# The last layer's gate: half of its contraction as seven block products

## The chip, the cores and the metric

The kernel runs on one core of one Trainium2 chip. The metric is the device time of one execution in microseconds. TensorE (PE in the profile) multiplies, VectorE (DVE) and ScalarE (ACT) do elementwise work, SyncE (SP) issues the transfers from memory.

## The reference

A two-layer decoder trunk on 512 tokens of 1024 features in float32. Layer 0 mixes tokens with a Mamba-2 SSD, layer 1 with HGRN2; each is followed by a layer norm, a squared-ReLU MLP and a second layer norm. What matters here is the end of a layer, with h of shape 512 x 1024:

```python
h = layer_norm(DEEPNORM_ALPHA * h + sq_relu_mlp(h, mlp_w1[i], mlp_w2[i]), ln_g[i, 1], ln_b[i, 1])
x = h + jax.nn.sigmoid(h @ ple_w_gate[i]) * (p[i] @ ple_w_proj[i])
```

The gate is a product of 512 x 1024 by 1024 x 1024, the projection one of 512 x 256 by 256 x 1024. The result of the last layer is the output.

## The kernel before

Tokens are cut into four chunks of 128 (c), features of the contraction into eight blocks of 128 (k), outputs into two halves of 512 (h), so that one PSUM bank holds 128 tokens x 512 outputs. Every float32 operand is split into a rounded part and a rest (`split`, `transpose_split`: a cast on ACT, line 113 or 242, and a subtraction on DVE, line 116 or 243), and `mm3` multiplies three times: hi·hi, hi·lo, lo·hi (lines 120 to 122). Weights come in units of 128 x 1024, two blocks k of one output half. `unit` takes one of three raw buffers, loads it on SP's queue (line 106), and splits it into one of six pairs whi, wlo.

The MLP's second product and a value projection of layer 1 already use the scheme of seven products for a 2 x 2 block product (`block_product`, `values4`). Sums of weight blocks (`weight_sums`, lines 333 to 341) are made by DVE in buffers r, of which there are eight; sums of token blocks are made from a plain copy of the turned rows (lines 551 to 564, `put` in lines 522 to 525).

The order on each engine is made by a scheduler that takes the instructions in the order of the code, moved ahead by the offsets of `high_priority` (LEAD = 100, SOON = 40 instructions), as their operands and buffers come free in its own model of time. Each engine then works through its list in order. Loops are unrolled.

The stage around the change, in `mlp_and_gate` for the last layer: the MLP's last block product fills acc, the rows of 512 tokens. `norm(3)` returns three things: `chunk(c)`, which normalises 128 tokens (`layer_norm`, lines 213 to 224), `transpose_split` for a chunk (two groups of four 128 x 128 transposes into the single bank pt, line 238, then the cast and the subtraction), and the row sums. Chunks 0 and 1 are normalised after the fifth product, chunks 2 and 3 after the last, in the last layer's case with no raised priority for chunks 2 and 3. Then lines 474 to 512 run the gate: for h = 0 all four projections of p first (line 482), with chunk 1's transposes between them, and for each chunk 24 matmuls into a bank pj (line 493) with the transposes of chunks 2 and 3 set between those of chunks 0 and 1. Each bank is followed by a sigmoid on ACT (line 496), a multiply by the projection and an add to acc on DVE (lines 503 and 506), and the store of 128 x 512 outputs (line 508). For h = 1 each chunk's projection comes right before its 24 matmuls; the last chunk's comes behind them, in two pieces of 256 columns, so that the last multiply, add and store are short.

Of the kernel before, what the change touches and what calls it, by code (L numbers as in the profile page):

```python
# [9 lines left out]
F32R = mybir.dt.float32r  # L10
# [34 lines left out]
def trunk(ctx: ExitStack, tc, a):  # L45
# [43 lines left out]
    def tmp(tag, shape, dt=F32):  # L89
        return mk(phase[0], shape, tag, dt, bufs=phase[2].get(tag, 1))  # L90
# [137 lines left out]
    def behind(ins):  # L228
        return tc.issue_after(ins.ins) if ins is not None else nullcontext()

    def transpose_split(src, dst, c, apart):

        sl = slice(c * P, (c + 1) * P)
        for q in range(2):
            pt = bank(psm, "pm") if apart and q else bank(pst, "pt")
            for j in range(4):
                k = 4 * q + j
                nc.tensor.transpose(pt[:, j * P : (j + 1) * P], src[:, k * P : (k + 1) * P], ident)  # L238
            v = pt.rearrange("p (j t) -> p j t", j=4)
            h = dst.hi[q][:, :, sl]  # L240
            with tc.high_priority(offset=LEAD if apart else SOON):
                nc.scalar.copy(h, v)
                turned_last[:] = [nc.vector.tensor_sub(dst.lo[q][:, :, sl], v, f32(h))]
            yield

# [34 lines left out]
                for c in range(NCH):  # L280
                    out_part(units, 4, xs, c, h, first, scale)

    def norm(i):
# [9 lines left out]
        return h_s, chunk, lambda c: transpose_split(acc[:, c, :], h_s, c, c == 3 and i % 2 == 0), sums  # L293

# [49 lines left out]
    def block_product(w, blk, lead, first, after=None, turns=None, sums=None, low=None):  # L344
# [41 lines left out]
        for f in (p1, p7, p6, p4, p5, p2, p3) if after else (p1, p2, p6, p7, p5, p4, p3):  # L386
# [4 lines left out]
                after(2), after(3)  # L391
            yield

    def mlp_and_gate(layer, h_s, last):
# [36 lines left out]
        for g, period in enumerate(PERIODS):  # L431
            if g < 4:
                tiles = hidden(g)
            if g > 0:
                if g == 4:
                    h_s, after, turned, sums = norm(2 * layer + 1)
# [11 lines left out]
        x_n = None if last else Split(8)  # L448
        rows = None if last else [tmp("blk", [P, 2, 4, 256]) for _ in range(2)]
        late = []  # L450

        def turn(h, c):

            sl = slice(c * P, (c + 1) * P)
            pt = bank(pst, "pt")
            for j in range(4):
                nc.tensor.transpose(pt[:, j * P : (j + 1) * P], acc[:, c, h * 512 + j * P : h * 512 + (j + 1) * P], ident)
            v = pt.rearrange("p (j t) -> p j t", j=4)
            hh = x_n.hi[h][:, :, sl]
            nc.scalar.copy(hh, v)  # L460
            nc.scalar.copy(rows[c // 2][:, h, :, c % 2 * P : (c % 2 + 1) * P], v)
            nc.vector.tensor_sub(x_n.lo[h][:, :, sl], v, f32(hh))

        pps = {}

        def proj(c, pu, chunk=None, cs=slice(0, T)):

            ps = pps[c] = bank(*((psj, "pj") if c > 1 and pps else (psy, "py%d" % (c % 2))))
            sl = slice(c * P, (c + 1) * P) if chunk is None else slice(chunk * P, (chunk + 1) * P)
            for k in range(2):  # L470
                ks = slice(k * 512 + cs.start, k * 512 + cs.stop)
                mm3(ps[:, cs], p_s[0][:, k, sl], p_s[1][:, k, sl], pu[0][:, ks], pu[1][:, ks], k == 0, k == 1)

        for h in range(2):
            pu = unit(a[f"wp_{layer}"][h])
            gu = [unit(a[f"wg_{layer}"][4 * h + j]) for j in range(4)]
            for c in range(NCH):
                sl = slice(c * P, (c + 1) * P)
                if h == c == 0:
                    turns = turned(1)  # L480
                    for i in range(NCH):
                        proj(i, pu)
                        if i in (1, 2):
                            next(turns)
                end = last and h == 1 and c == NCH - 1
                if h == 1 and not end:
# [9 lines left out]
                nc.scalar.activation(sg, pg, AF.Sigmoid)  # L496
                for i in range(2 if end else 1):
                    n = 256 if end else 512
                    cs = slice(i * n, (i + 1) * n)
                    if end:  # L500
                        proj(i, pu, c, cs)
                    pp = pps.pop(i if end else c)[:, cs]
                    nc.vector.tensor_mul(sg[:, cs], pp, sg[:, cs])  # L503
                    fs = slice(h * 512 + i * n, h * 512 + (i + 1) * n)
                    d = acc[:, c, fs]
                    nc.vector.tensor_add(d, sg[:, cs], d)
                    if last:
                        nc.sync.dma_start(a["out"][c * P : (c + 1) * P, fs], d)
                while late:
                    late.pop(0)()  # L510
                if not last:
                    late.append(lambda h=h, c=c: turn(h, c))
        return x_n, rows, late

    def values4(xs, rows, late):
# [791 lines left out]
```

## Time and profile before

| | us |
|---|---|
| median of 3 runs | 1415.1 (1414.85 to 1415.71) |
| the profiled execution | 1415.16 |
| its span, first to last instruction | 1413.4 |
| the last layer's gate, first projection to last matmul | 1351.3 to 1409.4 |

The profile is of one execution. Times in its rows count from the start of the span. A row of a timeline gives start, duration, engine, line of the kernel, operation, output<-inputs and shapes. A row of a group gives a count, the busy time, the mean in ns of one, and the idle time of the engine just before, with what ended it. PEld is the load of the stationary operand, which runs beside the matmuls.

### The profile page before, as it was taken

The page shows a single profiled execution, that of the slowest core. Times are in us where ns is not written, and L with a number is a line of the kernel's source. Part 1 is how long each engine was busy: PE and PEld are TensorE (multiplying, and loading weights), DVE is VectorE, ACT ScalarE, POOL GpSimd, SP SyncE. Part 2 cuts the span into 40 slices and gives each one's busy share as a digit, 9 for nine tenths or more (in the row PEclk, how much of TensorE's full clock was granted, in tenths as well). Part 3 has the DMA queues.
Part 4 walks back from the last instruction along what each step waited for, and adds up shares of the span by engine and source line. Part 5 has one row for each costly group of instructions (what it writes and reads, how often), then busy time and mean ns, then how long its engine had stood idle before and what let it go on. Part 6 is the DMA issues. An engine that isn't in the chain of part 4 may idle for free.

```text
span 1413.4 us, 20324 instructions
## 1 busy us (share of the span) xinstructions
PE 1408.5 (100%) x8013; PEld 1170.9 (83%) x8013; DVE 1057.1 (75%) x1759; ACT 750.7 (53%) x1132; POOL 1.9 (0%) x12
## 2 busy tenths in 40 slices
PE   9999999999999999999999999999999999999998
PEld 7888888888988888888888888888888888888887
DVE  7989687698977668677986577678785857667873
ACT  6766465573354444545555547655555454544641
POOL 0000000000000000000000000000000000000000
PEclk9999999999999999999999999999999999999999
DMA  8433333234434444444621421222163444444231
GB/s 304 140 120 117 108 119 107 88 100 143 151 114 134 149 136 147 137 147 164 214 85 49 134 91 61 76 91 90 44 241 105 153 145 134 149 135 162 91 119 45
DMA packets 49391, 178.02 MB, mean 126 GB/s; under 512 B 5520, under 2 KB 6288, under 8 KB 49168
## 3 DMA queue, kind: packets, MB, share of 16 engines
q1 hardware_dynamic: 49296, 176.73, 37.9%
q8 instruction: 63, 1.03, 0.3%
q14 instruction: 32, 0.26, 0.1%
HBM read 174.54 MB, written 2.16 MB: 125 GB/s over the span
## 4 chain that ended last, share of the span: by engine, by line
PE 99%; DMA 0%; DVE 0%; issue 0%; DVEq 0%
PE pj L120 25%; PE pj L121 25%; PE pj L122 25%; PE py L120 5%; PE py L122 5%; PE py L121 5%; PE py L749 1%; PE pt L238 1%; PE py L1018 1%; PE pm L766 1%; PE pm L714 1%; PE py L1144 1%; PE pt L702 0%; PE py L1146 0%; PE py L1083 0%; PE py L675 0%
## 5 line engine op out<-in xcount | busy, mean ns | idle before, releaser
L113 ACT CAST whi<-raw 128x1024 fp32r<-128x1024 f32 x222 | 233.2, 1051 | 331.8 <-PE pj L121 241.8
L120 PE MATMUL pj<-b,whi 128*128 128x512 f32 (+1 forms) x990 | 378.7, 383 | 0.0
L122 PE MATMUL pj<-b,wlo 128*128 128x512 f32 (+1 forms) x990 | 376.7, 381 | 0.0
L121 PE MATMUL pj<-b,whi 128*128 128x512 f32 (+1 forms) x990 | 376.6, 381 | 0.0
L116 DVE TENSOR_TENSOR wlo<-raw,whi 128x1024 fp32r<-128x1024 f32 x222 | 270.2, 1221 | 136.9 <-ACT whi L113 134.6
L121 PEld LDWEIGHTS pj<-b,whi 128*128 128x128 f32 x990 | 186.3, 188 | 34.5 <-issue 0.9
L122 PEld LDWEIGHTS pj<-b,wlo 128*128 128x128 f32 x990 | 186.2, 188 | 34.5
L120 PEld LDWEIGHTS pj<-b,whi 128*128 128x128 f32 x990 | 186.1, 188 | 34.2
L122 PE MATMUL pj<-whi,b 128*128 128x512 f32 x544 | 213.4, 392 | 0.0
L120 PE MATMUL pj<-whi,b 128*128 128x512 f32 x536 | 213.0, 397 | 0.0
L121 PE MATMUL pj<-wlo,b 128*128 128x512 f32 x536 | 210.3, 392 | 0.0
L122 PEld LDWEIGHTS pj<-whi,b 128*128 128x128 f32 x544 | 102.2, 188 | 21.1
L120 PEld LDWEIGHTS pj<-whi,b 128*128 128x128 f32 x536 | 100.8, 188 | 20.3 <-ACT b L1165 0.3
L121 PEld LDWEIGHTS pj<-wlo,b 128*128 128x128 f32 x536 | 100.7, 188 | 19.8 <-issue 0.2
L113 ACT CAST whi<-r 128x1024 fp32r<-128x1024 f32 x72 | 75.7, 1053 | 67.7 <-PE pj L122 38.5
L116 DVE TENSOR_TENSOR wlo<-r,whi 128x1024 fp32r<-128x1024 f32 x72 | 87.7, 1220 | 21.6 <-ACT whi L113 20.9
L122 PE MATMUL py<-whi,b 128*128 128x512 f32 (+1 forms) x250 | 97.0, 388 | 0.0
L121 PE MATMUL py<-wlo,b 128*128 128x512 f32 x224 | 87.2, 389 | 0.0
L120 PE MATMUL py<-whi,b 128*128 128x512 f32 x224 | 87.1, 390 | 0.0
L643 DVE SCALAR_TENSOR_TENSOR cv<-pj,cst,cv 128x509 f32<-128x509 f32 (+2 forms) x66 | 48.9, 745 | 10.5 <-ACT cv L640 9.7
L122 PEld LDWEIGHTS py<-whi,b 128*128 128x128 f32 x250 | 46.9, 188 | 9.7
L120 PEld LDWEIGHTS py<-whi,b 128*128 128x128 f32 x224 | 42.0, 188 | 9.2 <-DVE sg L503 0.3
(316 smaller groups left out, 1848.0 us busy)
## 6 DMA issues: line engine op xcount, KB each, us to landing
raw<-in_w SPq DMA_DIRECT2D x112, 512.0 KB, 3.4
r<-in_w SPq DMA_DIRECT2D x64, 512.0 KB, 3.9
raw<-in_wssd SPq DMA_DIRECT2D x36, 512.0 KB, 4.0
a<-csd SPq DMA_DIRECT2D x16, 512.0 KB, 4.1
raw<-in_wso SPq DMA_DIRECT2D x16, 512.0 KB, 3.4
raw<-in_wg SPq DMA_DIRECT2D x16, 512.0 KB, 3.5
raw<-in_whq SPq DMA_DIRECT2D x16, 512.0 KB, 3.5
raw<-in_whvg SPq DMA_DIRECT2D x14, 512.0 KB, 3.4
```

The costliest lines, as they stand in the source:

```text
L113: nc.scalar.copy(hi[:, :n], f)
L116: nc.vector.tensor_sub(lo[:, :n], f, f32(hi[:, :n]))
L120: nc.tensor.matmul(out, sh, mh, start=start, stop=False, **kw)
L121: nc.tensor.matmul(out, sh, ml, start=False, stop=False, **kw)
L122: nc.tensor.matmul(out, sl, mh, start=False, stop=stop, **kw)
L238: nc.tensor.transpose(pt[:, j * P : (j + 1) * P], src[:, k * P : (k + 1) * P], ident)
L643: nc.vector.scalar_tensor_tensor(cv[:, d:], ps[:, : T - d], convw[:, i, k : k + 1], cv[:, d:], ALU.mult, ALU.add)
L714: nc.tensor.matmul(pst_[:, c * P : (c + 1) * P], btok[:, c, :], xw[:, c].rearrange("p h q -> p (h q)"), start=True, stop=True)
L749: mm = nc.tensor.matmul(yds[0][64 * r : 64 * r + 64, sl], xdt[:, 2 * c + r, :], m[:, r, sl], start=True, stop=True)
L766: mm = nc.tensor.matmul(yo[:, c * P : (c + 1) * P], pv[:, c - 1].rearrange("p h q -> p (h q)"), cm[:, c * P : (c + 1) * P], start=True, st ...
L1018: nc.tensor.matmul(pcs[r][bs, at : at + n], kk[r][:, ts], qs, start=True, stop=True)
L1144: nc.tensor.matmul(po[:, sl], scs[r][:, c, :], v(c, r), start=True, stop=c == 0)
```

## The change

The last layer leaves `mlp_and_gate` for a function of its own, `last_gate`. Of the gate's contraction (1024 features) the first half, k = 0 to 3, is done as a 2 x 2 block product: tokens in halves i of 256, these 512 features in quarters q of 256, outputs in halves of 512. With tokens a11, a12, a21, a22 (token half, feature quarter) and weights b11, b21 (h = 0), b12, b22 (h = 1) it forms

- t3 = b22 - b12, t1 = b12 - b11, t2 = b22 - t1, t4 = b21 - t2 (the code holds b12, b22 in t12, t22),
- s1 = a21 + a22, s3 = a11 - a21, s2 = s1 - s3, s4 = a12 - s2 (each written over one of the four kept blocks),

and the seven products a11·b11, a12·b21, s3·t3, s2·t2, a22·t4, s1·t1 and s4·b22. A product is two banks of 6 matmuls. The second half of the contraction, k = 4 to 7, is added by 12 plain matmuls to a bank of each chunk and output half (`rest`). Partial banks are copied by ACT to tiles in SBUF ("cells") and added there by DVE. The units b11, b21 are loaded twice, once to be split and once for the sums; thirteen units are loaded instead of ten.

For the token sums, `transpose_split` also copies the first four turned blocks of a chunk, unsplit, to a tile `kept` (ACT, from pt). The normalisation of chunks 2 and 3 of the last layer gets the offset SOON. The order of tokens in the second output half is 2, 3, 0, 1; the end is again cut into two pieces of 256 columns, now of chunk 1. Cut to its core:

```diff
             with tc.high_priority(offset=LEAD if apart else SOON):
                 nc.scalar.copy(h, v)
+                if keep is not None and q == 0:
+                    nc.scalar.copy(keep[:, c // 2, :, c % 2 * P : (c % 2 + 1) * P], v)
                 turned_last[:] = [nc.vector.tensor_sub(dst.lo[q][:, :, sl], v, f32(h))]
...
-            with tc.high_priority(offset=LEAD if c == 3 and i % 2 == 0 else SOON if c < 2 or i % 2 == 0 else 0):
+            with tc.high_priority(offset=LEAD if c == 3 and i % 2 == 0 else 0 if c > 1 and i == 1 else SOON):
                 layer_norm(i, c, gb, sums)
...
+    def last_gate(wp, wg, h_s, p_s, kept, turned):
+        t12, t22, t3, t11, t21 = (tmp("r", [P, 1024]) for _ in range(5))
+        with tc.high_priority(offset=SOON):
+            for t, n in ((t12, 4), (t22, 5), (t11, 0), (t21, 1)):
+                nc.sync.dma_start(t, wg[n])
+            nc.vector.tensor_sub(t3, t22, t12)
...
+        pu = unit(wp[0])
+        b11, b21 = unit(wg[0]), unit(wg[1])
+        us = [unit(wg[2]), unit(wg[3])]
+        turns = turned(1)
+        for c in range(NCH):
+            ps = bank(psj, "pj")
+            proj(ps, c, pu)
+            nc.scalar.copy(cell(c), ps)
+            if c in (1, 2):
+                next(turns)
+        nc.vector.tensor_sub(t11, t12, t11)
+        nc.vector.tensor_sub(t22, t22, t11)
+        nc.vector.tensor_sub(t21, t21, t22)
+        x = [bank(psy, "py%d" % u) for u in range(2)]
+        turns = turned(2)
+        for u in range(2):
+            part(x[u], direct(0, 0), b11, u, True)
+            nc.scalar.copy(cell(4 + u), x[u])
+            next(turns)
+        turns = turned(3)
+        for u in range(2):
+            z = bank(psj, "pj")
+            part(z, direct(0, 1), b21, u, True, False)
+            if u:
+                next(turns)
+            rest(z, u, us, False)
+            if not u:
+                next(turns)
+            nc.vector.tensor_add(cell(4 + u), z, cell(4 + u))
+            final(u, 0, cell(4 + u), [(cell(u), whole)])
...
+        with tc.high_priority(offset=LEAD):
+            nc.vector.tensor_add(a22, a21, a22)
+            nc.vector.tensor_sub(a21, a11, a21)
+            put(0, a21)
+            nc.vector.tensor_sub(a11, a22, a11)
+            put(1, a11)
+            put(2, a22)
+            nc.vector.tensor_sub(a12, a12, a11)
+            put(3, a12)
+        t3, t2, t4, t1 = split(t3), split(t22), split(t21), split(t11)
+        y = [bank(psj, "pj") for _ in range(2)]
+        for u in range(2):
+            part(y[u], summed(0), t3, u, True)
+            nc.scalar.copy(cell(8 + u), y[u])
+        for u in range(2):
+            part(x[u], summed(1), t2, u, False)
+            nc.scalar.copy(cell(6 + u), x[u])
+        for u in range(2):
+            part(y[u], direct(1, 1), t4, u, False, False)
+            rest(y[u], 2 + u, us, False)
+            nc.vector.tensor_add(cell(6 + u), y[u], cell(6 + u))
+            final(2 + u, 0, cell(6 + u), [(cell(2 + u), whole)])
+        for u in range(2):
+            part(x[u], summed(2), t1, u, False)
+            nc.vector.tensor_add(cell(8 + u), x[u], cell(8 + u))
...
+                    kept = tmp("blk", [P, 2, 4, 256]) if last else None
+                    h_s, after, turned, sums = norm(2 * layer + 1, kept)
```

Behind these come the second half's units (wp[1], wg[6], wg[7], wg[5]), the projections and plain matmuls of chunks 2 and 3, and for chunk 0 and then chunk 1 the product s4·b22 with its plain matmuls and the projection. `final` is the sigmoid, the multiply, the add and the store of lines 496 to 508 before.

More of the change, by code (lines that the diff above doesn't have):

```diff
@@ L229, in behind, with transpose_split @@
         return tc.issue_after(ins.ins) if ins is not None else nullcontext()
-    def transpose_split(src, dst, c, apart):
+    def transpose_split(src, dst, c, apart, keep=None):
         sl = slice(c * P, (c + 1) * P)
@@ L281, in out_project, with norm @@
                     out_part(units, 4, xs, c, h, first, scale)
-    def norm(i):
+    def norm(i, keep=None):
         gb = ln_params(i)
@@ L289, in chunk @@
         def chunk(c):
-            with tc.high_priority(offset=LEAD if c == 3 and i % 2 == 0 else SOON if c < 2 or i % 2 == 0 else 0):
+            with tc.high_priority(offset=LEAD if c == 3 and i % 2 == 0 else 0 if c > 1 and i == 1 else SOON):
                 layer_norm(i, c, gb, sums)
-        return h_s, chunk, lambda c: transpose_split(acc[:, c, :], h_s, c, c == 3 and i % 2 == 0), sums
+        return h_s, chunk, lambda c: transpose_split(acc[:, c, :], h_s, c, c == 3 and i % 2 == 0, keep), sums
     def half_blocks(blk, z0, z1, p):
@@ L392, in block_product, with proj, direct, summed @@
             yield
+    def last_gate(wp, wg, h_s, p_s, kept, turned):
[4 more added lines that the diff above has]
+            nc.vector.tensor_sub(t3, t22, t12)
+        pairs = [mk(b8, [P, 2, 4, 256], "b8", F32R) for _ in range(2)]
+        cells = [mk(b8, [P, 4, T], "b8") for _ in range(3)]
+        cell = lambda n: cells[n // 4][:, n % 4, :]
+        tok = lambda c: slice(c * P, (c + 1) * P)
+        def proj(ps, c, pu, cs=slice(0, T)):
+            for k in range(2):
+                ks = slice(k * 512 + cs.start, k * 512 + cs.stop)
+                mm3(ps[:, cs], p_s[0][:, k, tok(c)], p_s[1][:, k, tok(c)], pu[0][:, ks], pu[1][:, ks], k == 0, k == 1)
+        def direct(i, q):
+            return lambda k, u: (h_s.h(2 * q + k, tok(2 * i + u)), h_s.l(2 * q + k, tok(2 * i + u)))
+        def summed(n):
+            t, ks = pairs[n // 2], 2 * (n % 2)
+            return lambda k, u: (t[:, 0, ks + k, tok(u)], t[:, 1, ks + k, tok(u)])
+        def part(ps, x, w, u, start, stop=True):
+            for k in range(2):
+                ks = slice(k * 512, (k + 1) * 512)
+                mm3(ps, *x(k, u), w[0][:, ks], w[1][:, ks], start and k == 0, stop and k == 1, skip_group_check=True)
+        def rest(ps, c, us, start):
+            for k in range(4, 8):
+                ks = slice((k % 2) * 512, (k % 2 + 1) * 512)
+                hi, lo = us[k // 2 - 2]
+                mm3(ps, h_s.h(k, tok(c)), h_s.l(k, tok(c)), hi[:, ks], lo[:, ks], start and k == 4, k == 7, skip_group_check=True)
+        def final(c, h, g, pp):
+            sg = tmp("sg", [P, T])
+            nc.scalar.activation(sg, g, AF.Sigmoid)
+            for i, (ps, cs) in enumerate(pp):
+                if callable(ps):
+                    ps = ps()
+                nc.vector.tensor_mul(sg[:, cs], ps[:, cs], sg[:, cs])
+                fs = slice(h * 512 + cs.start, h * 512 + cs.stop)
+                nc.vector.tensor_add(acc[:, c, fs], sg[:, cs], acc[:, c, fs])
+                nc.sync.dma_start(a["out"][tok(c), fs], acc[:, c, fs])
+        whole = slice(0, T)
+        pu = unit(wp[0])
[28 more added lines that the diff above has]
+            final(u, 0, cell(4 + u), [(cell(u), whole)])
+        a11, a12, a21, a22 = (kept[:, i, 2 * q : 2 * q + 2, :] for i in range(2) for q in range(2))
+        def put(n, f):
+            t, ks = pairs[n // 2], slice(2 * (n % 2), 2 * (n % 2) + 2)
+            nc.scalar.copy(t[:, 0, ks, :], f)
+            nc.vector.tensor_sub(t[:, 1, ks, :], f, f32(t[:, 0, ks, :]))
+        with tc.high_priority(offset=LEAD):
[23 more added lines that the diff above has]
+            nc.vector.tensor_add(cell(8 + u), x[u], cell(8 + u))
+        pu = unit(wp[1])
+        us = [unit(wg[6]), unit(wg[7])]
+        b22 = unit(wg[5])
+        pp = [bank(psj, "pj") for _ in range(2)]
+        for u in range(2):
+            proj(pp[u], 2 + u, pu)
+        for u in range(2):
+            g = bank(psj, "pj")
+            rest(g, 2 + u, us, True)
+            nc.vector.tensor_add(cell(8 + u), g, cell(8 + u))
+            final(2 + u, 1, cell(8 + u), [(pp[u], whole)])
+        part(x[0], summed(3), b22, 0, False, False)
+        rest(x[0], 0, us, False)
+        ps = bank(psj, "pj")
+        proj(ps, 0, pu)
+        final(0, 1, x[0], [(ps, whole)])
+        part(x[1], summed(3), b22, 1, False, False)
+        rest(x[1], 1, us, False)
+        def piece(p, tag, cs):
+            def make():
+                ps = bank(p, tag)
+                proj(ps, 1, pu, cs)
+                return ps
+            return make, cs
+        final(1, 1, x[1], [piece(psj, "pj", slice(0, 256)), piece(psm, "pm", slice(256, 512))])
@@ L446, in mlp_and_gate @@
                 next(tiles if op == "T" else products)
-        x_n = None if last else Split(8)
-        rows = None if last else [tmp("blk", [P, 2, 4, 256]) for _ in range(2)]
+        if last:
+            return last_gate(a[f"wp_{layer}"], a[f"wg_{layer}"], h_s, p_s, kept, turned)
+        x_n = Split(8)
+        rows = [tmp("blk", [P, 2, 4, 256]) for _ in range(2)]
         late = []
@@ L484, in mlp_and_gate @@
                             next(turns)
-                end = last and h == 1 and c == NCH - 1
-                if h == 1 and not end:
+                if h == 1:
                     proj(c, pu)
@@ L496, in mlp_and_gate @@
                 nc.scalar.activation(sg, pg, AF.Sigmoid)
[L497 to L508, printed above, removed]
+                nc.vector.tensor_mul(sg, pps.pop(c), sg)
+                d = acc[:, c, h * 512 : (h + 1) * 512]
+                nc.vector.tensor_add(d, sg, d)
                 while late:
                     late.pop(0)()
-                if not last:
-                    late.append(lambda h=h, c=c: turn(h, c))
+                late.append(lambda h=h, c=c: turn(h, c))
         return x_n, rows, late
```

9 lines of the change are left out of this document (4 added, 5 removed).

## The prediction

> **What bounds the kernel now.** I read the page's busy line first, then its chain that ended last, then the busy time by stretches around the stage that changes, then the matmul engine's timeline inside it.
>
> ```profile
> PE 1408.5 (100%) x8013; PEld 1170.9 (83%) x8013; DVE 1057.1 (75%) x1759; ACT 750.7 (53%) x1132; POOL 1.9 (0%) x12
> PE 99%; DMA 0%; DVE 0%; issue 0%; DVEq 0%
> ```
>
> The first row says that PE (TensorE) is never idle. As ends of matmuls are modelled, it could still hide small gaps, so the second row matters more: the chain that ended last is PE for 99% of the span. Time can only leave this kernel as PE work, and it comes back only as a wait of PE. The busy time by stretches (stretch, length, then busy us and counts of PE, PEld, DVE, ACT, POOL, then granted clock, DMA share, GB/s):
>
> ```profile
> 1330.00:1350.80 20.80, 20.80 (x94) 17.18 (x93) 17.31 (x31) 10.89 (x18) 0.00 (x0) 1.00 0.61 197
> 1350.80:1361.00 10.20, 10.20 (x53) 8.38 (x52) 9.70 (x19) 6.80 (x16) 0.00 (x0) 1.00 0.43 145
> 1361.00:1371.00 10.00, 10.00 (x53) 8.23 (x52) 6.73 (x9) 4.23 (x7) 0.00 (x0) 1.00 0.24 80
> 1371.00:1381.00 10.00, 10.00 (x48) 8.18 (x47) 5.46 (x8) 3.94 (x6) 0.00 (x0) 1.00 0.14 52
> 1381.00:1391.00 10.00, 10.00 (x46) 8.29 (x45) 4.65 (x6) 2.11 (x3) 0.00 (x0) 1.00 0.07 26
> ```
>
> The last layer's gate starts near 1351. The clock is 1.00, DMA has room, and DVE (VectorE) is nearly full in the first ten microseconds (9.70 of 10.20) and half free later. The change puts new work on DVE and ACT (ScalarE); the question is how much of it is due inside the full part.
>
> ```profile
> 1351.32 0.48 PE L120 MATMUL pj<-whi,a 128*128 128x512 f32 x1
> ...
> 1369.49 0.61 PE L238 MATMUL pt<-cst,acc 128*128 128x128 f32 x4
> ...
> 1371.32 0.39 PE L120 MATMUL pj<-whi,b 128*128 128x512 f32 x1
> 1371.54 0.61 PE L238 MATMUL pt<-cst,acc 128*128 128x128 f32 x4
> ...
> 1372.23 0.39 PE L122 MATMUL pj<-whi,b 128*128 128x512 f32 x1
> ...
> 1382.02 0.39 PE L120 MATMUL py<-whi,a 128*128 128x512 f32 x1
> ...
> 1407.63 0.39 PE L122 MATMUL pj<-whi,b 128*128 128x512 f32 x1
> ...
> 1409.17 0.28 PE L122 MATMUL py<-whi,b 128*128 128x256 f32 x1
> ```
>
> A matmul is shown with 0.39 us, but neighbours overlap, so its price is the distance from start to start. Between the rows at 1382.02 and 1407.63 the code issues three chunks of 6 + 24 matmuls and 24 of the last, 114 in all, so 113 distances: 25.61 / 113 = 0.2266 us each. A group of four transposes costs 1372.23 - 1371.32 = 0.91 less two distances, 0.46 us.
>
> **What the change removes.** Before, the gate has 4 chunks x 2 output halves x 8 k x 3 = 192 matmuls. After, seven products of 2 chunks x 2 k x 3 are 84, and the plain half of K is 8 banks x 4 k x 3 = 96, together 180. The projection of p keeps 42 full-width matmuls and 12 of 256 columns, and the eight groups of transposes stay. PE loses 12 matmuls: 12 x 0.2266 = **2.72 us**, 0.19% of the span. More than that the change cannot give as PE work.
>
> The Trainium skill prices a matmul otherwise: TensorE: Matmul & The Clock Gate, section "Back-to-back issue gap", states about 131 ns for a sustained stream at 512 columns. By it the gain would be an estimated 12 x 0.131 = 1.6 us; the distance measured above is 226.6 ns, the trace disagrees and decides.
>
> **What it adds, and when it is due.** Until the first product of sums PE has work that needs only tokens 0 to 255: 24 projections, 12 + 12 matmuls of the products a11·b11 and a12·b21, 24 of the plain half, 72 in all, as many as the old stage had (24 + 48) before it needed chunk 2. With seven transpose groups among them that is over at 1351.32 + 72 x 0.2266 + 7 x 0.46 = 1370.9. Then PE needs the split t3, and the split of a11 - a21, for which chunks 2 and 3 must be normalised, turned and kept.
>
> ```profile
> 1355.04 1.22 DVE L116 TENSOR_TENSOR wlo<-raw,whi 128x1024 fp32r<-128x1024 f32 x1
> 1360.71 1.21 DVE L116 TENSOR_TENSOR wlo<-raw,whi 128x1024 fp32r<-128x1024 f32 x1
> 1361.83 1.28 DVE L224 SCALAR_TENSOR_TENSOR acc<-acc,lnrs,b 128x1024 f32<-128x1024 f32 x1
> 1364.02 1.28 ACT L496 ACT_TABLE_LOAD   x1 [2.00 <-PE pj L122]
> 1365.31 0.60 ACT L496 ACTIVATE sg<-pj 128x512 f32<-128x512 f32 x1
> 1365.94 0.69 DVE L503 TENSOR_TENSOR sg<-py,sg 128x512 f32<-128x512 f32 x1 [1.04 <-ACT sg L496]
> 1367.15 0.68 DVE L506 TENSOR_TENSOR acc<-sg,acc 128x512 f32<-128x512 f32 x1
> L243 DVE TENSOR_TENSOR b<-pt,b 128x512 fp32r<-128x512 f32 x8 | 5.5, 687 | 2.2 <-ACT b L242 2.2
> L242 ACT CAST b<-pt 128x512 fp32r<-128x512 f32 x8 | 4.7, 583 | 7.3 <-PE pt L238 7.3
> L113 ACT CAST whi<-raw 128x1024 fp32r<-128x1024 f32 x222 | 233.2, 1051 | 331.8 <-PE pj L121 241.8
> L542 ACT COPY a<-py 128x512 f32<-128x512 f32 x4 | 2.4, 588 | 1.6 <-PE py L122 1.6
> L305 ACT CAST b<-b x48: 614/622/627, 397.5 to 1312.7; 128x512 fp32r<-128x512 f32 x48
> ```
>
> DVE by work. From 1350.8 to 1371.0 it is busy 9.70 + 6.73 = 16.4 of 20.2 us. Of that, the two weight splits at 1355.04 and 1360.71 (second-half units, which now come later) and the first output at 1365.94 and 1367.15 leave the stretch: 2.4 + 1.4. So 12.6 stays and 7.6 is room. Due by 1370.9 are t3's split (1.22), two token sums and one split of 512 columns (0.69 each, by the L243 row): 3.3. The four weight sums are 4 x 1.22 = 4.9 more, 8.2 together, 0.6 too much if all of them fall here. The next rows say that they need not.
>
> ```profile
> 1304.13 1.22 DVE L116 TENSOR_TENSOR wlo<-r,whi 128x1024 fp32r<-128x1024 f32 x1
> r<-in_w SPq DMA_DIRECT2D x64, 512.0 KB, 3.9
> L326 SPq DMA_DIRECT2D r<-in_whvg x8: 327/328/328, 654.0 to 675.6; - x8
> L341 DVE TENSOR_TENSOR r<-r,r x2: 1215/1216/1218, 719.5 to 722.4; 128x1024 f32<-128x1024 f32 x2
> 705.00:711.00 6.00, 6.00 (x32) 4.93 (x31) 6.00 (x11) 4.68 (x13) 0.00 (x0) 1.00 0.29 90
> 717.00:723.00 6.00, 6.00 (x34) 4.98 (x33) 5.90 (x9) 1.77 (x3) 0.00 (x0) 1.00 0.00 0
> ```
>
> The buffers r of the MLP's weight sums come free from 1305 on. The four loads of 512 KB (0.33 us of SP's queue each) land 3.9 us after issue, in a stretch where DVE has 20.80 - 17.31 = 3.5 us idle: room for two sums before the gate, leaving 2.4. Layer 0 shows the same pattern: its value stage's weights were loaded at 654 to 676, long before the code reaches them, and summed as late as 722, within layer 0's gate. There DVE was full (6.00 and 5.90 of 6.00), while PE kept its pace. So the sums take what DVE leaves over. As these loads use r, not the three raw buffers, they queue behind no unit that waits for one. The stage loads 13 units of 512 KB instead of 10; at a DMA share of 0.07 to 0.61 I take them at nothing, and at up to 3.9 us each if SP's order put a needed one last.
>
> DVE by order. The two splits gone and the chunks' normalisation raised in priority bring the L224 of chunk 2 from 1361.83 to about 1360.6. The groups of transposes share one bank and follow each other every 1371.54 - 1369.49 = 2.05 us at best; from 1362.9 on that puts chunk 3's first group at 1367.0 instead of 1369.49. Behind it stand the transposes (0.61), the cast (0.58), the kept copy (0.59), two sums (1.37), a cast (0.62) and a split (0.69): 1371.5, **0.6 us after** PE asks. Cost from both sides: nothing, if DVE takes a11 - a21 first; 3.0 us, if chunk 3's group stays at 1369.49. I take 0.5, nearer to the early case, since the splits that stood in the way are gone.
>
> ACT gets the ten copies of banks to cells (0.59 each), four kept copies, four casts of sums (0.62) and three more casts of weights (1.05): 13.9 us over the gate, some 8.6 of it before 1371. There it was busy 11.0 of 20.2 and loses two casts and the first sigmoid with its table load, 4.0 us: 15.6 of 20.2 is covered. Uncovered, each late copy holds a bank: cost inside the 3.0 above.
>
> Beyond 1371 DVE owes, within the 24 matmuls (5.4 us) before t4 is due, one sum, one split, t2, t4 and the last turn: 4.5 us. It fits if the outputs of tokens 0 to 255 (4.1) and the sums for later products (2.1) wait. After that DVE was busy 4.65 of 10 us and less. The end is as before: 12 half-width matmuls, two multiplies, two adds, the last stores, about 4 us from the last matmul (1409.17) to the end of the span that I leave unchanged.
>
> **Sum.** 2.72 gone, 0.5 back: -2.2 us. The profiled execution took 1415.16 us with a span of 1413.4, 1.8 us around it; the median of the runs is 1415.1, so both give **1412.9 us**. A measurement of this kernel can tell about 0.2% (2.8 us) from no change; the whole ceiling lies just below that.
>
> **Rivals.** *Late chunk 3.* The chain to the first sum keeps its old place at 1369.49, as when the first sigmoid's table load (1.28, then 0.60) falls between the kept copy and the first cast. PE waits 3.0 us: 1415.1 - 2.7 + 3.0 = 1415.4, no change. For it: L243 waited for ACT 2.2 us in all already; against: the sigmoid now comes behind 54 matmuls, not 48. The Trainium skill, ScalarE: Activation LUTs, section "What ACT_TABLE_LOAD costs", adds a drain to about 2.66 us; by it the wait would be an estimated 1.4 longer. The trace has the sigmoid start straight behind the 1.28.
>
> *DVE becomes the bound (slower).* The new work runs in the order of the code: no weight sum before the gate (0.6 over at 1370.9), and outputs and later sums ahead of t2 and t4: 4.5 + 4.1 + 2.1 = 10.7 in 5.4 us. PE waits 0.6 + 5.3 = 5.9: 1415.1 - 2.7 + 5.9 = 1418.3. It decides once PE's waits pass 2.7; it is over 0.2% from 5.6 on. For it: DVE's 9.70 of 10.20; against: layer 0's stage above.
>
> *More than the ceiling.* From 1351.32 to 1382.02 stand 120 matmuls and seven groups, 27.2 + 3.2 = 30.4 of 30.7 us: 0.3 of hidden slack. If no wait appears and that goes too: 1412.1, over 0.2% faster. The change not doing what it says would show as a count of matmuls; the code leaves no room for it.
>
> **How the numbers follow.** Forecast 0.45 (1412.2 to 1413.8 by itself, a seventh of it at the lower edge just past 0.2%), late chunk 0.25 (same), DVE bound 0.17 (slower), more than the ceiling 0.13 (faster). So faster 0.13 + 0.07 = 0.20, same 0.38 + 0.25 = 0.63, slower 0.17. The range goes from 1411.8, a little under the last rival, to 1416.8, halfway from late chunk to DVE bound; it leaves out most of the latter and a little below.
>
> **What would show it.** 12 fewer matmuls of 512 columns, at 0.227 us apart; weight sums (r from r) before 1351; the first product with a sum as stationary operand near 1371 with at most 1 us of PE idle before it, and none before t2, t4, t1; the same 4 us behind the last matmul. I am wrong if PE idles over 1 us in front of one of the seven products (whose releaser tells ACT, DVE or DMA), or if the MLP's products before 1351 are disturbed by the early loads and sums.

## The result and the profile after

| | before | after |
|---|---|---|
| median | 1415.09 us (1414.75 to 1415.71, 5 runs) | 1422.08 us (1421.70 to 1423.64, 5 runs) |
| ratio after / before | | 1.0053 [1.0038, 1.0067] |
| profiled execution, its span | 1415.16, 1413.4 | 1423.64, 1421.5 |

The kernel became slower by 7.0 us. (Ratios and their intervals come from all runs, not from the two medians, so they can differ from the quotient of the medians in the fourth decimal.) From the page of after, the busy time and the chain that ended last:

```profile
PE 1410.2 (99%) x8001; PEld 1171.4 (82%) x8001; DVE 1074.3 (76%) x1782; ACT 762.9 (54%) x1153; POOL 1.9 (0%) x12
PE 96%; DVE 2%; ACT 1%; DMA 1%; issue 0%; DVEq 0%; ACTq 0%
```

The 12 matmuls are gone (8001, not 8013), yet PE's busy time grew by 1.7 us, and DVE and ACT stand in the chain, where before it was PE nearly alone. Fewer matmuls and more busy time point to a lower clock. The busy time by stretches, in the columns of the prediction's rows, and what PE waited for in the whole execution (total, times, longest):

```profile
1350.80:1361.00 10.20, 10.10 (x47) 7.68 (x46) 10.20 (x20) 7.19 (x17) 0.00 (x0) 1.00 0.33 104
1361.00:1371.00 10.00, 9.68 (x48) 7.78 (x49) 8.60 (x11) 8.07 (x13) 0.00 (x0) 1.00 0.00 0
1371.00:1381.00 10.00, 5.12 (x19) 3.54 (x18) 8.09 (x14) 5.26 (x10) 0.00 (x0) 0.69 0.08 28
1381.00:1391.00 10.00, 10.00 (x37) 8.05 (x37) 4.72 (x6) 4.76 (x7) 0.00 (x0) 0.80 0.23 79
```

```profile
PE pt L238 <- DVE b L245: 3.7, 2, 2.5
PE pj L120 <- ACT b L479: 1.2, 1, 1.2
PE py L120 <- DVE lnsum L372: 0.9, 1, 0.9
...
```

The third stretch holds the damage: PE is busy for 5.12 of 10 us, and the granted clock, 1.00 in these stretches of before, is 0.69 there and 0.80 in the next. Line 238 is the transposes, 245 the subtraction that empties their bank, 479 the cast of a token sum, 451 (below) the copy of a projection to its cell. The wait for line 372 lies in layer 0, at 703 us, where the source is unchanged; it comes and goes between the kernels below that share this part (0.9 here and in one other, 1.0 and 0.3 in two, not listed in the rest), so I don't count it to the seven products. It makes the profiled execution's difference larger than the 7.0 us of the medians, and it is one reason why the stage starts at another time in each kernel: the first projection stands at 1352.24 here, at 1351.32 in before. Places in two kernels are therefore compared by their distance from the first projection. PE's timeline in the stage:

```profile
1357.94 0.60 PE L238 MATMUL pt<-cst,acc 128*128 128x128 f32 x4
1361.33 0.50 PE L120 MATMUL pj<-whi,b 128*128 128x512 f32 x1 [0.41 <-ACT b L451]
1365.10 0.60 PE L238 MATMUL pt<-cst,acc 128*128 128x128 f32 x4
...
1369.95 0.65 PE L238 MATMUL pt<-cst,acc 128*128 128x128 f32 x4
...
1371.84 0.40 PE L122 MATMUL pj<-whi,b 128*128 128x512 f32 x1
1373.44 0.66 PE L238 MATMUL pt<-cst,acc 128*128 128x128 f32 x4 [1.20 <-DVE b L245]
1376.59 1.11 PE L238 MATMUL pt<-cst,acc 128*128 128x128 f32 x4 [2.49 <-DVE b L245]
1378.89 0.80 PE L120 MATMUL pj<-whi,b 128*128 128x512 f32 x1 [1.20 <-ACT b L479]
...
1385.02 0.39 PE L122 MATMUL py<-whi,b 128*128 128x512 f32 x1
```

The last product that needs no token sum is issued at 1371.84, the first with a sum as stationary operand at 1378.89. Between them PE does only chunk 3's two groups of transposes. The matmul's own 0.23 and the two groups at 0.46 taken off, 7.05 - 0.23 - 0.92 = **5.9 us** is lost to the wait. (The rows show 1.20 + 2.49 + 1.20 = 4.9 us of it as idle. The rest is mostly the second group, which at the lower clock takes 1.11 us instead of 0.46.) From 1378.89 to 1385.02 stand 14 distances in 6.13 us, most of them 0.43 each, where 14 x 0.2266 would be 3.17: **3.0 us** more lost at a lower clock in this execution. The sum is -2.7 + 5.9 + 3.0 + 0.4 (line 451) = +6.6 of the 7.0 measured.

Now the chain behind the 5.9. DVE first, then ACT, in the same stage:

```profile
1358.71 1.28 DVE L223 SCALAR_TENSOR_TENSOR acc<-acc,lnmv,a 128x1024 f32<-128x1024 f32 x1
...
1361.31 2.46 DVE L224 SCALAR_TENSOR_TENSOR acc<-acc,lnrs,b 128x1024 f32<-128x1024 f32 x2
1363.68 0.69 DVE L245 TENSOR_TENSOR b<-pt,b 128x512 fp32r<-128x512 f32 x1
...
1372.70 0.68 DVE L245 TENSOR_TENSOR b<-pt,b 128x512 fp32r<-128x512 f32 x1
...
1375.24 0.69 DVE L483 TENSOR_TENSOR blk<-blk 128x512 f32<-128x512 f32 x1 [0.66 <-ACT blk L244]
1375.85 0.68 DVE L245 TENSOR_TENSOR b<-pt,b 128x512 fp32r<-128x512 f32 x1
1376.45 0.68 DVE L484 TENSOR_TENSOR blk<-blk 128x512 f32<-128x512 f32 x1
```

```profile
1370.13 1.28 ACT L434 ACT_TABLE_LOAD   x1
1371.43 0.63 ACT L434 ACTIVATE sg<-b 128x512 f32<-128x512 f32 x1
1371.96 0.57 ACT L242 CAST b<-pt 128x512 fp32r<-128x512 f32 x1
...
1374.61 0.59 ACT L244 COPY blk<-pt 128x512 f32<-128x512 f32 x1
...
1377.74 0.58 ACT L242 CAST b<-pt 128x512 fp32r<-128x512 f32 x1 [2.00 <-PE pt L238]
1378.22 1.66 ACT L479 CAST b<-blk 128x512 fp32r<-128x512 f32 x3
```

A group of transposes may start only when the group before it has left the bank pt: cast (242), for every other group the kept copy (244), and the subtraction (245). Four things delay that. Chunk 1's first group, turned at 1357.94, is released by the subtraction at 1363.68, behind 5 us of normalisation of chunks 2 and 3, so the next group starts at 1365.10, 7.2 us later, and chunk 2's first group (1367.15) is late with it. Chunk 2's second group, turned at 1369.95, has its cast only at 1371.96, behind the first sigmoid and its table load. The sum a21 + a22 (line 483, at 1375.24), which has the raised priority LEAD, goes ahead of the subtraction (1375.85) that frees the bank for chunk 3's second group, and it waits for a copy on ACT first. And PE's order has both groups of chunk 3 ahead of the first product of sums, and ACT's order has the second group's cast (1377.74) ahead of the sum's (1378.22), though that product needs only the first group. The last two are read from the rows; no run changes either of them alone.

### The profile page after: what moved, and what is told of

It is laid out like the page before. It is cut to its first block, busy times and chain, and to the rows that moved or that the text cites. A ratio compares the mean times of both kernels' runs of the same rounds, so it can differ in the third digit from the quotient of the medians.

```text
span 1421.5 us, 20350 instructions
## 1 busy us (share of the span) xinstructions
PE 1410.2 (99%) x8001; PEld 1171.4 (82%) x8001; DVE 1074.3 (76%) x1782; ACT 762.9 (54%) x1153; POOL 1.9 (0%) x12
## 4 chain that ended last, share of the span: by engine, by line
PE 96%; DVE 2%; ACT 1%; DMA 1%; issue 0%; DVEq 0%; ACTq 0%
PE pj L120 24%; PE pj L121 24%; PE pj L122 24%; PE py L120 5%; PE py L122 5%; PE py L121 5%; PE py L884 1%; PE pt L238 1%; PE py L1153 1%; PE pm L901 1%; PE pm L849 1%; DVE wlo L116 1%; PE py L1279 1%; PE pt L837 0%; DMA raw<-in_w 0%; PE py L1281 0%
## 5 line engine op out<-in xcount | busy, mean ns | idle before, releaser
L122 PE MATMUL pj<-whi,b 128*128 128x512 f32 x528 | 208.0, 394 | 0.0
L120 PE MATMUL pj<-whi,b 128*128 128x512 f32 x508 | 203.3, 400 | 1.6 <-ACT b L479 1.2
L121 PE MATMUL pj<-wlo,b 128*128 128x512 f32 x508 | 200.4, 394 | 0.0
L122 PEld LDWEIGHTS pj<-whi,b 128*128 128x128 f32 x528 | 99.8, 189 | 20.5
L113 ACT CAST whi<-r 128x1024 fp32r<-128x1024 f32 x76 | 79.9, 1053 | 68.4 <-PE pj L122 38.6
L120 PEld LDWEIGHTS pj<-whi,b 128*128 128x128 f32 x508 | 96.1, 189 | 21.7 <-ACT b L479 1.6
L121 PEld LDWEIGHTS pj<-wlo,b 128*128 128x128 f32 x508 | 96.2, 189 | 18.9 <-issue 0.2
L116 DVE TENSOR_TENSOR wlo<-r,whi 128x1024 fp32r<-128x1024 f32 x76 | 92.6, 1220 | 21.8 <-ACT whi L113 21.3
L122 PE MATMUL py<-whi,b 128*128 128x512 f32 x260 | 101.5, 390 | 0.0
L120 PE MATMUL py<-whi,b 128*128 128x512 f32 x248 | 96.8, 392 | 0.0
L121 PE MATMUL py<-wlo,b 128*128 128x512 f32 x248 | 96.8, 390 | 0.0
L122 PEld LDWEIGHTS py<-whi,b 128*128 128x128 f32 x260 | 49.0, 188 | 10.2
L120 PEld LDWEIGHTS py<-whi,b 128*128 128x128 f32 x248 | 46.7, 188 | 10.4 <-ACT b L242 0.5
```

The lines of the kernel that those rows point to most:

```text
L113: nc.scalar.copy(hi[:, :n], f)
L116: nc.vector.tensor_sub(lo[:, :n], f, f32(hi[:, :n]))
L120: nc.tensor.matmul(out, sh, mh, start=start, stop=False, **kw)
L121: nc.tensor.matmul(out, sh, ml, start=False, stop=False, **kw)
L122: nc.tensor.matmul(out, sl, mh, start=False, stop=stop, **kw)
```

## The experiments

Two theories. **Chain**: the wait is a chain of single steps through bank pt, ACT's order and PE's order; loosen a link and PE's wait shrinks, with the same work on DVE. **DVE's work**: the gate now simply has more DVE work than fits, the prediction's rival for a slower kernel; loosening a link gains little. (The first expectation has a third: the raised priority alone is the loss.) The first four kernels tell these apart. All are edits of after; before, run beside them, had a median of 1414.85 us.

**The raised priority undone.**

```diff
-            with tc.high_priority(offset=LEAD if c == 3 and i % 2 == 0 else 0 if c > 1 and i == 1 else SOON):
+            with tc.high_priority(offset=LEAD if c == 3 and i % 2 == 0 else SOON if c < 2 or i % 2 == 0 else 0):
```

> The changed kernel with one edit undone: chunks 2 and 3 of the last norm are normalised at their old priority. Theory one, the chain (transposes of chunks 1 to 3 through the single bank pt, with their cast, copy and subtraction, up to the first split of a token sum): in the profile after, chunk 1's second group came 7.2 us after its first, because DVE normalised chunks 2 and 3 in between; with the old priority that gap shrinks to about 3.5 us, but chunk 3 is normalised 2 to 3 us later, so the wait before the first product of sums changes by less than 2 us: 1420 to 1423. Theory two, DVE's amount of work: the amount is the same, so no change, 1422. Theory three, the raised priority alone is the loss: 1415 or less.

Measured 1419.31 us, ratio 1.0031 [1.0019, 1.0044]: 2.8 us better than after, and between the forecasts: less than the chain's 1420 to 1423, far from the 1415 of the raised priority alone. The edit matters more than I thought, but it is one link of several. PE in its profile:

```profile
1369.71 0.61 PE L238 MATMUL pt<-cst,acc 128*128 128x128 f32 x4
1373.18 0.66 PE L238 MATMUL pt<-cst,acc 128*128 128x128 f32 x4 [2.86 <-DVE b L245]
1375.03 0.80 PE L120 MATMUL pj<-whi,b 128*128 128x512 f32 x1 [1.19 <-ACT b L479]
```

From the first projection (1350.53 here) chunk 3's first group stands at 19.18 us, in after at 21.20, and the first product of sums at 24.50 instead of 26.65. Normalising chunks 2 and 3 sooner made them turn later, since it took DVE from the subtraction that frees the bank. The rest of the wait stays, and so does the slow stretch behind it.

**The first two sigmoids, with the table load, held behind the cast of the second sum.**

```diff
-            final(u, 0, cell(4 + u), [(cell(u), whole)])
...
-            put(1, a11)
+            held = put(1, a11)
...
+        with tc.issue_after(held.ins):
+            for u in range(2):
+                final(u, 0, cell(4 + u), [(cell(u), whole)])
```

(`put` returns its cast.)

> The changed kernel with the first two sigmoids (and with them the table load and the outputs of tokens 0 to 255) held behind the casts of the first two token sums on ACT. Theory one, the chain: the table load and sigmoid (1.9 us on ACT) and the first output (1.4 us on DVE) leave the path to the first split, so PE waits 2 to 3 us less, 1419 to 1420; if the clock falls only after a longer idle time, some 3 us more come back, 1416. Theory two, DVE's amount of work: 1421 to 1422, as nothing is taken away.

Measured 1420.34 us, ratio 1.0038 [1.0023, 1.0053]: 1.7 us better, between the forecasts of the two theories (1419 to 1420, 1421 to 1422). The 1.20 us wait in front of chunk 3's first group is gone, the 2.49 in front of its second and 1.19 in front of the product of sums are still there.

**The second group of each chunk in the other bank.**

```diff
-            pt = bank(psm, "pm") if apart and q else bank(pst, "pt")
+            pt = bank(psm, "pm") if (apart or keep is not None) and q else bank(pst, "pt")
```

> The changed kernel with the second group of transposes of each chunk in the bank pm, which is idle until the end, so that two groups can be under way. Theory one, the chain: a group no longer waits for the subtraction of the one before; chunk 3's first group, which came at 1373.4 in the profile after, can come near 1368 to 1370, and the last one no longer stands before the product; PE's 5.9 us of waiting go to 0 to 2 and the clock stays up: 1412.5 to 1415. Theory two, DVE's amount of work: 1420 to 1422.

Measured 1414.06 us, ratio 0.9995 [0.9985, 1.0004]: 8.0 us better than after by one condition. Its last groups, the step ahead of the first sum and the busy time of the stage:

```profile
1368.35 0.60 PE L238 MATMUL pm<-cst,acc 128*128 128x128 f32 x4
...
1369.68 1.28 ACT L434 ACT_TABLE_LOAD   x1
...
1371.51 1.64 ACT L479 CAST b<-blk 128x512 fp32r<-128x512 f32 x3
...
1372.16 0.50 PE L120 MATMUL pj<-whi,b 128*128 128x512 f32 x1 [0.90 <-ACT b L479]
```

```profile
1350.80:1391.00 40.20, 39.30 (x185) 32.19 (x184) 37.69 (x55) 27.60 (x48) 0.00 (x0) 1.00 0.17 57
```

The last group is turned at 1368.35 instead of 1376.59. One wait of 0.90 is left, ahead of the sum's cast, which stands behind the table load and a sigmoid. DVE does more of its work in the same stretch (37.69 of 40.20 us busy; in after the four stretches hold 10.20 + 8.60 + 8.09 + 4.72 = 31.6) and PE still loses far less. The theory of too much DVE work falls here as the cause of the 7 us. The clock is 1.00.

**The token sums made from tokens 0 to 255 alone**, so that they wait for no late chunk. (This kernel leaves tokens 256 to 511 out of the sums, so it does not compute the gate; it serves to time the dependency.)

```diff
-                if keep is not None and q == 0:
-                    nc.scalar.copy(keep[:, c // 2, :, c % 2 * P : (c % 2 + 1) * P], v)
+                if keep is not None and q == 0 and c < 2:
+                    for i in range(2):
+                        nc.scalar.copy(keep[:, i, :, c * P : (c + 1) * P], v)
```

> The changed kernel, but the kept copies of chunks 0 and 1 are written to both token halves of the kept tile and chunks 2 and 3 are not kept: the token sums are made from tokens 0 to 255 alone, so they need not wait for chunks 2 and 3. The same number of instructions on every engine. Theory one, the chain: the first product of sums finds its operand ready, PE waits at most for the last transposes: 1412.4 to 1414, the ceiling of the twelve matmuls. Theory two, DVE's amount of work: PE still waits for splits, 1418 or more.

Measured 1413.92 us, ratio 0.9995 [0.9986, 1.0004]: 8.2 us better, no wait at the sums (one of 0.9 us for a projection's copy is left), DVE as busy as with two banks (37.9 of 40.2). The products, copies and additions are the same in number; only the dependency on the late chunks is gone. So the dependency costs the time, not the work.

**The clock.** In after and in the first two edits the clock fell during the wait and stayed low behind it; in the next two, with little wait, it did not. To separate the idle time from the wait, unread matmuls were put into it:

```diff
+        def fill(ins, n):
+            wb = bank(psm, "pm")
+            for _ in range(n):
+                with tc.issue_after(ins.ins):
+                    ins = nc.tensor.matmul(wb, p_s[0][:, 0, tok(0)], p_s[0][:, 0, :], start=True, stop=True, skip_group_check=True)
...
+        fill(end, 5)
+        fill(turn1, 10)
+        fill(turn2, 7)
```

Here `end` is the last independent matmul, `turn1` and `turn2` the last transposes of chunk 3's two groups.

> The kernel after, with 22 matmuls of 128x512 added that nothing reads (5 behind the last of the independent products, 10 behind the first group of chunk 3, 7 behind its second), so that PE works through most of its 5.9 us of waiting while the wait for the first token sum stays as long. Theory (the 0.426 us between matmuls after the wait come of the granted clock, which fell because PE stood still): clock 1.00 throughout, the 14 distances after the wait 0.227 again, 3.0 us back, so 1419.1 us (1418.5 to 1419.7). Rival (the slow matmuls come of something else after the wait, such as operands or banks): the distances stay 0.4 and the time 1421.5 or more.

Measured 1418.72 us, ratio 1.0030 [1.0018, 1.0041]: 3.4 us better than after for **22 matmuls more**. (Before had 1414.96 beside it.) PE of this kernel:

```profile
1376.99 0.39 PE L120 MATMUL pj<-whi,b 128*128 128x512 f32 x1
1377.22 0.39 PE L121 MATMUL pj<-wlo,b 128*128 128x512 f32 x1
```

Behind the filled wait the first product runs 0.23 apart. The wait itself remains: 3.8 us over before, against -2.7 + 5.9 + 0.4 = 3.6.

**Only the middle filled** (0, 10, 0).

> As the kernel with the filled stall, but only the 10 unread matmuls between the two groups of chunk 3; 1.4 us before them and 1.8 us behind them stay idle. If what lowers the clock is one long unbroken stretch without matmuls, none is left (longest 1.8 us), and the time is 1419.1 us (1418.5 to 1419.7) as with all 22. If it is the idle time summed over some 7 us (3.6 us remain), the clock falls again, wholly or in part: 1420.5 to 1422.

Measured 1418.95 us, ratio 1.0029 [1.0017, 1.0040], clock 1.00 in the profiled stage.

```profile
1372.17 0.66 PE L238 MATMUL pt<-cst,acc 128*128 128x128 f32 x4 [1.20 <-DVE b L245]
...
1377.16 0.51 PE L120 MATMUL pj<-whi,b 128*128 128x512 f32 x1 [1.19 <-ACT b L492]
```

With no idle stretch over 1.2 us the clock stays, although 2.6 us of idle time are left in all (0.18 more lies between these two).

**Only the ends filled** (5, 0, 7).

> The stall of the kernel after with 5 unread matmuls ahead of the first group of chunk 3 and 7 behind the second, none between the groups: one unbroken stretch of about 2.5 us without matmuls is left, with busy stretches on both sides. If 2.5 us alone lower the clock: distances of 0.4 behind it, 1421 to 1422. If the clock needs more idle time than that: 0.227 throughout and 1418.9 us (1418.3 to 1419.5), as with the whole stall filled.

Measured 1420.42 us, ratio 1.0039 [1.0025, 1.0053], before 1414.94 beside it. PE, and the windows of one microsecond (length, PE busy, granted clock, DMA share, GB/s):

```profile
1376.57 1.12 PE L238 MATMUL pt<-cst,acc 128*128 128x128 f32 x4 [2.49 <-DVE b L245]
1377.34 2.81 PE L437 MATMUL pm<-a 128*128 128x512 f32 x7
1379.98 0.39 PE L120 MATMUL pj<-whi,b 128*128 128x512 f32 x1
```

```profile
1375.00:1376.00 1.00, 0.00 (x0) 0.99 0.55 197
1376.00:1377.00 1.00, 0.43 (x2) 0.50 0.03 10
...
1379.00:1380.00 1.00, 1.00 (x5) 0.81 0.00 0
1380.00:1381.00 1.00, 1.00 (x6) 1.00 0.00 0
```

One gap of 2.5 us was enough: PE stands still from 1374.08, and the clock is 0.50 from 1375.98, 1.9 us into the gap, to 1379.38. (This is the profiled execution. Of the four, three had a mean granted clock of 0.999, which fits 3.4 us at one half, and one had 1.000, so it seems not to happen each time.) The four transposes take 1.12 us and the seven unread matmuls 0.38 each, so the first product comes at 1379.98, a microsecond later than in after; behind it the clock is full. The time lies between the two forecasts, since the unread matmuls took most of the slow stretch themselves.

**Towards a version that keeps the gain.** Two banks and the late sigmoids together:

> The two edits that each helped, together: second groups of transposes in the other bank, and the first two sigmoids with the table load held behind the cast of the second sum. Theory: with two banks the only wait left was 1.3 us for the first sum's cast behind table load and sigmoid; that goes, and all 12 matmuls fewer are kept: span 1413.4 - 2.7 = 1410.7, time 1412.4 to 1413.0. Rival (ACT and DVE have no room, the wait moves to the next product or to a later bank): 1413.8 to 1414.3, as with two banks alone.

Measured 1413.77 us, ratio 0.9995 [0.9986, 1.0004]. The forecast missed: PE waited 1.3 us again for a sum's cast. ACT was free, but on DVE the difference a11 - a21 stood behind the sum a21 + a22 and a subtraction of a second group. With the raised priority undone as well:

> The same two edits, and the raised priority of chunks 2 and 3 undone as well. Theory (with two banks the transposes no longer hang on the order of the normalisations): the same as with the two edits within 0.5 us, 1412.3 to 1413.3. Rival (chunk 3's normalisation, now later, holds the sums): PE waits 1 to 3 us again, 1413.8 to 1416.

Measured 1413.87 us, ratio 0.9992 [0.9984, 1.0001], with the same wait of 1.3 us: with two banks that priority no longer matters, as forecast, though the time lies in the range of the rival. Next, the first edits with the difference made first, in a tile of its own:

```diff
+            d = tmp("sg", [P, T]).rearrange("p (a b) -> p a b", a=2)
+            nc.vector.tensor_sub(d, a11, a21)
+            put(0, d)
             nc.vector.tensor_add(a22, a21, a22)
-            nc.vector.tensor_sub(a21, a11, a21)
-            put(0, a21)
```

> The kernel with two banks and the sigmoids behind the cast, and the difference a11 - a21 made first, into a tile of its own, ahead of the sum of a22 and a21; with the two edits before it the difference stood behind that sum and a split of the second group on DVE (sum ready at 1368.7 us, difference started at 1370.11, cast 1370.88, first product 1371.55, where PE ran out at 1370.3). Theory: the difference starts about 1.2 us sooner, PE waits 0.3 us or less, and the 12 matmuls fewer are kept nearly whole: span 1410.4 to 1411.0, time 1412.3 to 1413.1. Rival (ACT or DVE is late with the next sums, so the wait moves behind the first product): 1413.5 to 1414.0.

Measured 1413.68 us, ratio 0.9991 [0.9981, 1.0000]. The wait at the first sum is gone, but another appears, and the time is in the rival's range:

```profile
1378.00 0.50 PE L121 MATMUL pj<-wlo,a 128*128 128x512 f32 x1 [0.43 <-DVE wlo L116]
```

```profile
1340.00:1371.00 31.00, 31.00 (x153) 25.38 (x151) 30.54 (x50) 24.43 (x48) 0.00 (x0) 1.00 0.29 94
```

Now a weight split is late, and DVE (third pair) is busy 30.54 of 31.00 us ahead of it. That suggests DVE's work as the next bound. Two weight sums moved to POOL should show it:

```diff
-        nc.vector.tensor_sub(t22, t22, t11)
-        nc.vector.tensor_sub(t21, t21, t22)
+        nc.gpsimd.tensor_sub(t22, t22, t11)
+        nc.gpsimd.tensor_sub(t21, t21, t22)
```

> The kernel with the three edits (two banks, sigmoids behind the cast, difference first), and two of the weight sums (b12 and b11 less their neighbours, lines 455 and 456, 1.22 us each on DVE) made on POOL, which does nothing else here. In the kernel with the three edits DVE was busy 30.5 of 31 us from 1340 to 1371 and PE lost 0.3 us to a dozen short waits at the sums and 0.6 us to a weight split (line 116) at 1378. Theory (what is left is DVE's amount of work, now that the chain of the transposes is out of the way): 2.4 us less on DVE give 0.4 to 0.9 us back, 1412.7 to 1413.3. Rival (the rest hangs on the order of the instructions, or POOL's sums come so late, or hold up DVE so much, that they cost what they save): 1413.5 or more.

Measured 1416.12 us, ratio 1.0008 [0.9999, 1.0017]: 2.4 us worse than without it.

```profile
1335.21 4.56 DVE L116 TENSOR_TENSOR wlo<-raw,whi 128x1024 fp32r<-128x1024 f32 x2
...
1352.38 0.66 PE L238 MATMUL pt<-cst,acc 128*128 128x128 f32 x4 [1.61 <-DVE acc L224]
```

POOL took 3.26 us for each sum, DVE 1.22. Nor did DVE win time: while POOL worked, from 1335.43 to 1342.04, two weight splits on DVE took 4.56 us (2.35 in the kernel without this edit) and a third 1.96 instead of 1.22, together 2.95 us more, against the 2.44 taken off. The scheduler also reordered DVE: two splits and an addition now stand ahead of a normalisation (line 224), and PE waits 1.6 us for it. So the test says nothing clean about DVE's amount of work; what holds back the rest of the gain, 1.4 of the 2.7 us, stays open.

## Why the prediction was wrong

**What bounds the kernel, and the ceiling: right.** PE lost exactly 12 matmuls, and once the chain is loosened the stage is PE's again (39.30 of 40.20 us busy). The reckoned 2.72 us was not exceeded. The end behind the last matmul takes 4.3 us, as before. No kernel here came more than 1.3 us under before in the same session.

**DVE by work: right in the main.** Three of four weight sums were made before the gate; the first and the last of the three:

```profile
1333.63 1.22 DVE L402 TENSOR_TENSOR r<-r,r 128x1024 f32<-128x1024 f32 x1
...
1339.40 1.22 DVE L455 TENSOR_TENSOR r<-r,r 128x1024 f32<-128x1024 f32 x1
```

With the chain loosened, the same work came with waits of about a microsecond. That it costs nothing is not shown: the best kernel still lacks 1.4 of the 2.7 us, with DVE busy for 30.54 of 31.00 us ahead of a late split.

**DVE by order: the step that failed.** It put chunk 3's first group at 1367.0, 15.7 us behind the first projection, and the wait at 0.5 us, with 3.0 as the upper bound; the group came at 1373.44, 21.2 us behind it, and the wait was 5.9. Three errors are in it. The raised priority was booked as a gain; undoing it gave 2.8 us, since it goes ahead of the subtraction that frees the bank. Of the 5.5 us by which chunk 3's group was late, 3.3 were there at chunk 2's first group already (1367.15, reckoned 1362.9). The upper bound was the old place, 1369.49, as if an order that held before could only improve, though the change adds copies to the same bank and puts a table load in its way. And the sum's chain was counted from the first group alone; in the order that was built the second group stands between, on PE and on ACT, so that 1373.44 to 1378.89 is 5.45 us against the 4.5 reckoned.

**Late chunk 3** had a right link, the table load ahead of a cast of the chain, but not its size: without it 1.7 us came back, where the rival reckoned 3.0, and it was one link of several. Part of the 1.7, as of the 2.8 above, may be the clock, whose slow stretch was 6.8 us in both profiles and 10.2 in that of after. **DVE becomes the bound** gave the nearest time, 1418.3, and even the size of the wait, 5.9, but the two-bank kernel shows its mechanism to be wrong, since the same DVE work there goes with a wait of 0.90, so that the agreement is chance.

**A term that the sum lacked: the clock.** It took PE's price of 0.2266 us as fixed. A wait of PE has a second price behind it; here 3.0 us on top of 5.9. Without it the time would have been 1419, as the kernels with a filled wait show, still outside the range. **ACT covered: nearly.** The late copies to cells (line 451) cost the 0.41 us shown, inside the bound given.

## What to carry to other kernels

Before raising the priority of a producer, list what shares its engine with the step that frees the buffer of its consumer: in a chain through a single bank, the release is the urgent step. An algorithm that saves 12 matmuls by adding a dependency at the seam between two stages pays for every link of that chain, so lay it out step by step in the new order of each engine, not by the old places, before counting the gain. And price a wait of TensorE of some 2 us or more above its length, since the matmuls behind it may run at half the clock: here 1.9 us of standing still preceded a fall, and 1.6 us left the clock alone.

## What the runs showed of the hardware

The granted clock fell to one half during waits of PE, and it stayed low for stretches of a few lengths. From the windows of one microsecond of after (as above):

```profile
1374.00:1375.00 1.00, 0.09 (x1) 0.88 0.13 49
1375.00:1376.00 1.00, 0.00 (x0) 0.50 0.57 213
1384.00:1385.00 1.00, 1.00 (x3) 0.50 0.15 55
1385.00:1386.00 1.00, 1.00 (x6) 1.00 0.00 0
```

A share of 0.88 means a fall at 1374.76; the rise is at 1385.0, so 10.2 us. With the ends filled it was 3.4 us (1375.98 to 1379.38), with the old priority 6.8 (windows of 0.92 and 0.67 put it from 1373.84 to 1380.66): one, two and three times 3.4. The other executions need not show the same: of the five of after, three had a mean granted clock of 0.996, as the profiled one, and two had 0.998.

The Trainium skill, TensorE: Matmul & The Clock Gate, section "Part 1: The HAM clock gate", states a free-running window of 3413 ns and half the rate after an idle one. The lengths agree with the window. That the whole window must be idle doesn't agree: in the 3.41 us ahead of the fall PE stood still for 1.86 us in after (1.20 and the first 0.66 of the 2.49) and for 1.90 with the ends filled. The rule of the Trainium skill's section "HAM oscillation — how this bites in real kernels", on the same page, no idle gaps over about 3.4 us, is not a safe limit here: a single gap of 2.5 us lowered the clock. Idle stretches of 1.2 us left it at 1.00 in the kernel with the middle filled, and so did the 1.61 us in the kernel with sums on POOL. Where between these the limit lies, and how it hangs on the place of the window, wasn't tried.
